# A fourth block of the up projection with seven products for eight, and the remaining units one behind each of most of its steps

## The chip, the cores and the metric

The kernel runs on one core of a Trainium2 chip. Its time is the device time of one execution in microseconds (us). The engines of the core work side by side, each through its own list of instructions in order: TensorE (PE) does the matrix products, VectorE (DVE) and ScalarE (ACT) the elementwise work, GpSimd (POOL) and SyncE (SP) here mostly issue transfers (DMAs). They wait for each other by semaphores. Products accumulate in PSUM, in eight banks of 128x512 values; everything else lies in SBUF, with 128 partitions.

## The reference

One block of an encoder for 256 tokens and 2048 channels: a mixer (retention and latent attention), then an MLP with a squared ReLU. Only the MLP matters here:

```python
D_MODEL = 2048
SEQ = 256
D_FF = 4 * D_MODEL
...
        h = h + _mixer(u, positions, w_in[l], ret_norm_g[l], w_ret_o[l], q_a_norm_g[l],
                       w_q_b[l], kv_a_norm_g[l], w_kv_b[l], w_mla_o[l], w_out[l])
        z = _rmsnorm(h, norm_mlp_g[l]) @ w_up[l]
        h = h + jnp.square(jax.nn.relu(z)) @ w_down[l]
    return _rmsnorm(h, norm_f_g)
```

`w_up` has 2048 x 8192 values, so the up projection turns 256 tokens of 2048 channels into 256 tokens of 8192 hidden channels.

## The kernel before

**Numbers in two halves.** Every fp32 operand is split into a high and a low half in fp32r: ACT casts the value to the high half (`split`, L550), DVE subtracts it from the value and so gets the low half (L551). A product of two such operands is three matmuls: high by high, high by low, low by high. A weight therefore costs, once loaded, one cast on ACT and one subtraction on DVE before PE can use it.

**The up projection in two forms.** The hidden channels are computed in two ways.

A *unit* (`Unit`) yields 128 hidden channels for all 256 tokens. The weights stand in PE and the tokens stream through. It has two parts, of eight tiles of channels each; a part loads 512 KB of weights, splits them, and does eight matmuls 512 wide (L176, high weights by both halves of the tokens) and eight 256 wide (L180, low weights by high tokens). All go into one bank, `z`. After the second part ACT copies the bank out (L1266), DVE adds its halves (L1267), and two parts later ACT applies ReLU and squares (L1270, L1231); POOL issues the store of 128 KB to the hidden units' place in DRAM (`hid`, L1232).

A *block* yields 1024 hidden channels by seven products for eight (Strassen's scheme in Winograd's form on 2x2 blocks: two token halves, two column halves, pairs of channel tiles). It has eight *steps* (`Step`), one for each pair of channel tiles, j = 0 to 7. A step has four parts, 0 to 3. It loads 1 MB in two DMAs (`raw`, `sraw`), forms sums of the weights on DVE (L307, L316, L317, buffer `forms`), and splits four operands, one for each part: the raw pair, two sums each for parts 1 and 2, and one raw tile for part 3. The tokens stand in PE (from `hT`, or their combinations `hc`) and the weights stream. Parts 0 to 3 have two, two, two and one of the seven products, each product three matmuls (L333 to L335). The products add up over the eight steps in seven banks `zs`, numbered 1 to 7; part 0 adds to products 3 and 4, part 1 to 2 and 5, part 2 to 6 and 1, part 3 to 7. With seven of the eight banks held by a block, units and turns share the last one.

At the end of a block `s_end` evicts: four copies on ACT, of products 3, 5, 1 and 7 (L522 to L528, `zo`), and on DVE e = product 6 + copy of 3, f = product 2 - e, product 4 + f and copy of 5 + f (L520); three further operations of DVE follow some parts later. So bank 3 comes free with ACT's first copy, bank 5 with its second, bank 2 with DVE's second operation and bank 4 with its third. The outcome has tokens on partitions, so it is turned: four *turns* for a block (`turn`), each four 128x128 transposes on PE (L1284), a ReLU and a square on ACT and a store of 256 KB. They stand in the next block's steps, from its second step on ahead of part 1; those of the last block stand behind the last two units.

In the kernel before there are three blocks (`SU = 3`, 3072 channels) and 40 units (5120 channels).

**The order.** It is written by hand as a list of parts: three units first (`EARLY`), the blocks' steps with units between, two units last (`LATE`), then the down projection. Units go into *slots* behind part 1 or part 3 of a step; `use` says which slots get one. Before, 23 slots behind part 3 (all but the very last) have a unit, and 12 of the 24 slots behind part 1: the steps with even j. `stream` walks the list: ahead of the matmuls of part n it has the loads up to part n+6 and the preparation (sums, casts and splits) up to part n+4 recorded. Each engine keeps that order. So the copy of a unit's bank stands in ACT's list, and the addition after it in DVE's, behind the preparation of the next four parts, and both hold what is listed behind them until the unit's last matmul is done. The evictions of a block stand likewise behind the preparation of the four parts that follow its last part.

While the first block runs, DVE and ACT also make the remaining half of the combinations `hc` of the tokens (`MAKE`, lines L231 to L241 and a split), which its steps j = 4 to 7 need. These hold two of the five `raw` buffers while they are made.

The down projection then takes the hidden units from DRAM in pairs, those of the units first and those of the blocks after, in steps of the same kinds.

Of the kernel before, what the change touches and what calls it, by code (L numbers as in the profile page):

```python
# [27 lines left out]
CHUNK = 64  # L28
DFF = 8192
FT = DFF // P  # L30
SU = 3
SJ = KT // 2
ST = SU * 1024 // P
EARLY, LATE = 3, 2
AHEAD = 4
PAIRED = 6
MAKE = 7, 2 * EARLY + 18
SUMS = (4, 7, 10), (0, 1, 2)
MANUAL = {getattr(mybir.EngineType, n) for n in ('Activation', 'DVE', 'PE', 'SP', 'Pool')}
# [66 lines left out]
def block_kernel(ctx: ExitStack, tc: tile.TileContext, A):  # L106
# [50 lines left out]
    def wtile(kind, shape):  # L157
        uid[0] += 1
        dt, bufs = (F32, 5) if kind == "raw" else (F32R, 4)
        return wp.tile(shape, dt, tag=kind, bufs=bufs, name=f"{kind}{uid[0]}")  # L160
# [440 lines left out]
    for k in range(KT):  # L601
        t = lead0[:, N_VEC:] if k == 0 else wtile("raw", [P, LEAD])
# [674 lines left out]
    def turn(u, jj):  # L1277
        pT = atps(f"zt{u}{jj}")
        for j in range(2):
            kt = 2 * jj + j  # L1280
            for t in range(2):
                o = j * S + t * P
                src = zo[:, 0, 2 * t + kt // 4, kt % 4 * P : kt % 4 * P + P]
                PE.transpose(pT[:, o : o + P], src, ident)  # L1284
        square(4 * u + jj, pT)

    def step(u, j, qs):
        def end():
            sums = s_end(qs, zo[:, 0].rearrange("p (t c) n -> p t c n", t=2), zo[:, 1])
            next(sums)  # L1290
            later.extend([d, lambda: next(sums)] for d in SUMS[u == SU - 1])
            turns.extend(lambda jj=jj: turn(u, jj) for jj in range(4))
# [13 lines left out]
    early = [Unit(i, 0) for i in range(EARLY)]  # L1306
    parts = [(e, h) for h in range(2) for e in early]
    units = list(range(EARLY, FT - ST - LATE))
    slots = [(u, j, h) for u in range(SU) for j in range(SJ) for h in (1, 3)][:-1]
    whole = [t for t in slots if t[2] == 3]  # L1310
    room = len(units) - len(whole)
    halves = [t for t in slots if t[2] == 1]
    if room >= 0:
        use = set(whole) | {halves[i * len(halves) // room] for i in range(room)}
    else:
        use = {t for t in whole if t[1] != PAIRED or t[0] >= -room}
    for u in range(SU):
        qs = {}
        for j in range(SJ):
# [69 lines left out]
    def finish(half, t, c, n, lo=0, hi=512):  # L1389
        h = residual(half, t, c)[:, lo:hi]  # L1390
        ps = both[half].q[ROLE[t, c]][:, lo:hi]
        V.scalar_tensor_tensor(h, in0=ps, scalar=rh2[:, t : t + 1], in1=h, op0=ALU.mult, op1=ALU.add)

        def square():
            SC.activation(ps, h, AF.Square, accum_out=ssf[:, t, n : n + 1])

        return square
# [90 lines left out]
    with tc.manual_schedule(engines=MANUAL):  # L1488
        stream(parts, after)
        assert not later  # L1490
        for t in range(2):
            for c in range(2):
# [10 lines left out]
                else:  # L1503
                    halves = [finish(1, t, 1, 3, 0, 256)]
# [86 lines left out]
```

## Time and profile before

| what | value |
|---|---|
| time, median of 3 runs | 1566.04 us (1565.64 to 1566.29) |
| the profiled execution | 1566.54 us, its span 1564.8 us |
| PE busy | 1551.3 us (99%) |
| DVE busy | 1316.0 us (84%) |
| ACT busy | 962.6 us (62%) |
| POOL busy | 39.3 us (3%) |
| granted clock of PE, mean | 0.998 |
| from HBM read, to HBM written | 319.72 MB, 12.58 MB |

"Busy" counts the time in which at least one instruction of the engine is under way. In a timeline each row has the start in us from the span's start, the length, the engine, the line of the kernel, the operation, output<-inputs by the program's names (`lo<-raw,hi` is the subtraction that makes a low half), the shape, and xN where N such instructions follow each other; a bracket at the end gives the idle time ahead of it and what ended that. Lengths of matmuls overlap, so the time that one takes from its neighbours is the distance of two starts. The up projection runs from about 878 us, its first unit, to 1222 us.

### The profile page before, as it was taken

What the parts mean: (1) busy time and instruction counts of PE and PEld (TensorE: products, weight loads), DVE (VectorE), ACT (ScalarE), POOL (GpSimd) and SP (SyncE); (2) the same over time, 40 slices, a digit from 0 to 9 for tenths busy, and PEclk for the clock granted to TensorE, in tenths of its full rate; (3) what the DMA queues carried; (4) which work ended last, traced back from release to release, by engine and by line L of the source; (5) the groups of instructions that cost most, each with busy time, mean ns of one, the idle gap of its engine ahead of it and who ended that gap; (6) DMA issues with size and microseconds to landing.
All of it is one profiled execution on the core that took longest, in us unless ns stands there. A gap on an engine that the chain in (4) does not pass through costs nothing.

```text
span 1564.8 us, 21391 instructions
## 1 busy us (share of the span) xinstructions
PE 1551.3 (99%) x7655; PEld 1311.0 (84%) x7655; DVE 1316.0 (84%) x1787; ACT 962.6 (62%) x1416; POOL 39.3 (3%) x76
## 2 busy tenths in 40 slices
PE   9999999999999999999999999999999999999997
PEld 7888888888898888888888888888888888888886
DVE  7898877799976988976567689887978899989996
ACT  6645655566545667875445567676767766656664
POOL 0000000000000000000000000000000100000000
PEclk9999999999999999999999999999999999999999
DMA  9666755566656654444556657666675977686873
GB/s 319 207 203 208 230 164 161 159 201 206 206 168 220 213 197 143 157 136 161 185 206 211 236 196 247 214 226 232 207 249 188 376 265 245 237 304 211 266 255 115
DMA packets 107626, 333.70 MB, mean 213 GB/s; under 512 B 11264, under 2 KB 12160, under 8 KB 106496
## 3 DMA queue, kind: packets, MB, share of 16 engines
q1 hardware_dynamic: 104208, 318.71, 61.1%
q0 software_dynamic: 3168, 11.54, 1.9%
q10 hardware_dynamic: 144, 2.10, 0.4%
q8 instruction: 60, 0.98, 0.3%
q14 instruction: 46, 0.38, 0.1%
HBM read 319.72 MB, written 12.58 MB: 212 GB/s over the span
## 4 chain that ended last, share of the span: by engine, by line
PE 79%; DVE 1%; issue 1%; ACT 1%; DVEq 0%; POOLq 0%; POOL 0%; ACTq 0%
PE z L176 9%; PE dn L358 7%; PE dn L359 7%; PE dn L357 7%; PE z L180 5%; PE zs L333 2%; PE zs L334 2%; PE zs L335 2%; PE mo L214 2%; PE mo L215 2%; PE mo L217 2%; PE wo L214 2%; PE wo L215 2%; PE wo L217 2%; PE gm L357 2%; PE yr L358 2%
## 5 line engine op out<-in xcount | busy, mean ns | idle before, releaser
L551 DVE TENSOR_TENSOR lo<-raw,hi 128x1024 fp32r<-128x1024 f32 (+3 forms) x214 | 232.0, 1101 | 22.7 <-ACT hi L550 22.2
L169 DVE TENSOR_TENSOR lo<-raw,hi 128x1024 fp32r<-128x1024 f32 (+1 forms) x148 | 173.2, 1171 | 89.7 <-ACT hi L168 89.6
L168 ACT CAST hi<-raw 128x1024 fp32r<-128x1024 f32 (+1 forms) x148 | 149.6, 1011 | 155.9 <-PE mo L215 44.9
L550 ACT CAST hi<-raw 128x1024 fp32r<-128x1024 f32 (+3 forms) x214 | 200.0, 953 | 55.3 <-issue 9.5
L551 DVE TENSOR_TENSOR morelo<-raw,morehi 128x1024 fp32r<-128x1024 f32 (+1 forms) x118 | 127.1, 1098 | 18.8 <-ACT morehi L550 18.3
L550 ACT CAST morehi<-raw 128x1024 fp32r<-128x1024 f32 (+1 forms) x118 | 109.1, 949 | 10.5 <-issue 3.2
L550 ACT CAST hi<-forms 128x1024 fp32r<-128x1024 f32 x70 | 73.7, 1052 | 51.2 <-DVE forms L307 28.1
L176 PE MATMUL z<-hT,morehi 128*128 128x512 f32 x408 | 101.6, 391 | 0.0
L357 PE MATMUL dn<-hi,dd 128*128 128x512 f32 x230 | 89.6, 389 | 0.0
L359 PE MATMUL dn<-hi,dd 128*128 128x512 f32 x230 | 89.5, 389 | 0.0
L358 PE MATMUL dn<-lo,dd 128*128 128x512 f32 x230 | 89.5, 389 | 0.0
L551 DVE TENSOR_TENSOR lo<-forms,hi 128x1024 fp32r<-128x1024 f32 x70 | 85.0, 1221 | 5.3 <-ACT hi L550 4.9
L176 PEld LDWEIGHTS z<-hT,morehi 128*128 128x128 f32 x408 | 74.9, 188 | 14.4
L1266 ACT COPY hs<-z 128x512 f32<-128x512 f32 x40 | 23.5, 587 | 71.2 <-PE z L180 71.1
L357 PE MATMUL dn<-morehi,dd 128*128 128x512 f32 x156 | 60.7, 389 | 0.0
L358 PE MATMUL dn<-morelo,dd 128*128 128x512 f32 x156 | 60.7, 389 | 0.0
L359 PE MATMUL dn<-morehi,dd 128*128 128x512 f32 x156 | 60.7, 389 | 0.0
L180 PEld LDWEIGHTS z<-hT,morelo 128*128 128x128 f32 x408 | 55.6, 190 | 4.0
L176 PE MATMUL z<-hT,hi 128*128 128x512 f32 x232 | 57.9, 392 | 0.0
L180 PE MATMUL z<-hT,morelo 128*128 128x256 f32 x408 | 56.9, 282 | 0.0
L307 DVE TENSOR_TENSOR forms<-raw,sraw 128x1024 f32<-128x1024 f32 x46 | 56.1, 1219 | 0.3 <-DMA raw<-w_up_s 0.3
L358 PEld LDWEIGHTS dn<-lo,dd 128*128 128x128 f32 x230 | 43.2, 188 | 9.0
(500 smaller groups left out, 4193.9 us busy)
## 6 DMA issues: line engine op xcount, KB each, us to landing
raw<-w_down SPq DMA_DIRECT2D x106, 512.0 KB, 6.0
raw<-w_up SPq DMA_DIRECT2D x80, 512.0 KB, 5.1
raw<-w_rv SPq DMA_DIRECT2D x32, 512.0 KB, 4.8
raw<-w_rg SPq DMA_DIRECT2D x32, 512.0 KB, 4.3
raw<-w_gret SPq DMA_DIRECT2D x32, 512.0 KB, 4.4
raw<-w_ret_o SPq DMA_DIRECT2D x32, 512.0 KB, 5.0
raw<-w_gmla SPq DMA_DIRECT2D x32, 512.0 KB, 4.3
raw<-w_mla_o SPq DMA_DIRECT2D x32, 512.0 KB, 3.7
```

Source lines behind the costliest of these rows:

```text
L168: SC.copy(hi, raw)
L169: V.tensor_tensor(out=lo, in0=raw, in1=hi.bitcast(F32), op=ALU.subtract)
L176: PE.matmul(out, w[0][:, k], x.both(k0 + k), start=start and k == 0, stop=False)
L180: PE.matmul(out[:, :S], w[1][:, k], x.hi(k0 + k), start=False, stop=stop and k == n - 1)
L214: PE.matmul(out, x.hi(k0 + k, ts), w[0][:, k], start=start and k == 0, stop=False)
L215: PE.matmul(out, x.lo(k0 + k, ts), w[0][:, k], start=False, stop=False)
L217: PE.matmul(out, x.hi(k0 + k, ts), w[1][:, k], start=False, stop=stop and k == nk - 1)
L357: PE.matmul(q, ah, wh, start=start, stop=False)
L358: PE.matmul(q, ah, wl, start=False, stop=False)
L359: PE.matmul(q, al, wh, start=False, stop=self.left[f] == 0)
L550: SC.copy(hi, val)
L551: V.tensor_tensor(out=lo, in0=val, in1=hi.bitcast(F32), op=ALU.subtract)
```

## The change

The number of blocks goes from three to four (`SU`), so 4096 of the 8192 hidden channels come from blocks, in 32 steps, and 32 units are left instead of 40. Three of these stay first and two last; the other 27 are spread over the 31 slots behind part 3 of a step, and no unit stands behind part 1 any more. With whole division by 27 the slots that get none are numbers 7, 15, 23 and 30, counted from 0: behind the last steps of blocks 0, 1 and 2, and behind the seventh step of block 3.

```diff
-SU = 3
+SU = 4
 SJ = KT // 2
 ST = SU * 1024 // P
 EARLY, LATE = 3, 2
 AHEAD = 4
-PAIRED = 6
...
     units = list(range(EARLY, FT - ST - LATE))
-    slots = [(u, j, h) for u in range(SU) for j in range(SJ) for h in (1, 3)][:-1]
-    whole = [t for t in slots if t[2] == 3]
-    room = len(units) - len(whole)
-    halves = [t for t in slots if t[2] == 1]
-    if room >= 0:
-        use = set(whole) | {halves[i * len(halves) // room] for i in range(room)}
-    else:
-        use = {t for t in whole if t[1] != PAIRED or t[0] >= -room}
+    whole = [(u, j, 3) for u in range(SU) for j in range(SJ)][:-1]
+    use = {whole[i * len(whole) // len(units)] for i in range(len(units))}
```

The program up to the up projection keeps its order; line numbers are smaller by one there. In the rows below, `z` is a unit's bank, `zs` a block's, `zo` a block's evicted values, `hi`, `lo`, `morehi` and `morelo` the split weights; "waits" names the engines whose semaphore an instruction waits for ("Activation" is ACT).

PE's list where block 0 ends and block 1 begins, before: the last rows of the unit behind the last step, and then products 3, 4 and 2 of the new block.

```order
L180 MATMUL z14_9272<-hT0_7390,morelo1022_60_9214 128x256 x7
L176 MATMUL z14_9272<-hT1_7391,morehi1022_61_9223 128x512 [waits Activation_49]
L176 MATMUL z14_9272<-hT1_7391,morehi1022_61_9223 128x512 x7
L180 MATMUL z14_9272<-hT1_7391,morelo1022_61_9224 128x256 [waits DVE_49]
L180 MATMUL z14_9272<-hT1_7391,morelo1022_61_9224 128x256 x7
L333 MATMUL zs10333_9318<-morehi1023_62_9239,hT0_7390 128x512 [waits Activation_49]
L334 MATMUL zs10333_9318<-morehi1023_62_9239,hT0_7390 128x512
L335 MATMUL zs10333_9318<-morelo1023_62_9240,hT0_7390 128x512 [waits DVE_49]
L333 MATMUL zs10334_9319<-morehi1023_62_9239,hc0_7713 128x512 [waits Activation_49]
L334 MATMUL zs10334_9319<-morehi1023_62_9239,hc0_7713 128x512
L335 MATMUL zs10334_9319<-morelo1023_62_9240,hc0_7713 128x512
L333 MATMUL zs10332_9320<-hi1025_9253,hc0_7713 128x512 [waits DVE_49]
```

The same place in PE's list now: the last product of the old block, and at once products 3, 4 and 2 of the new one.

```order
L332 MATMUL zs9337_8325<-hi1001_8982,hT1_7391 128x512 [waits Activation_49]
L333 MATMUL zs9337_8325<-hi1001_8982,hT1_7391 128x512
L334 MATMUL zs9337_8325<-lo1002_8983,hT1_7391 128x512 [waits DVE_49]
L332 MATMUL zs10093_9068<-hi1003_9006,hT0_7390 128x512 [waits Activation_49]
L333 MATMUL zs10093_9068<-hi1003_9006,hT0_7390 128x512
L334 MATMUL zs10093_9068<-lo1004_9007,hT0_7390 128x512 [waits DVE_49]
L332 MATMUL zs10094_9069<-hi1003_9006,hc0_7713 128x512 [waits Activation_49]
L333 MATMUL zs10094_9069<-hi1003_9006,hc0_7713 128x512
L334 MATMUL zs10094_9069<-lo1004_9007,hc0_7713 128x512
L332 MATMUL zs10092_9070<-morehi1004_53_9018,hc0_7713 128x512 [waits DVE_49]
L333 MATMUL zs10092_9070<-morehi1004_53_9018,hc0_7713 128x512
L334 MATMUL zs10092_9070<-morelo1004_53_9019,hc0_7713 128x512
```

The unit is gone from between; product 3 now waits for ACT, product 4 for ACT and product 2 for DVE right behind the last matmul of the old block.

DVE's list there, before, from the splits of that unit to the first split behind the evictions (the four rows L520 that write `zo`):

```order
L551 TENSOR_TENSOR morelo1022_60_9214<-raw1016_9161,morehi1022_60_9213 128x1024
L551 TENSOR_TENSOR morelo1022_61_9224<-raw1019_9184,morehi1022_61_9223 128x1024
L307 TENSOR_TENSOR forms_8108<-raw1022_9209,sraw1022_9210 128x1024
L551 TENSOR_TENSOR morelo1023_62_9240<-sraw1022_9210,morehi1023_62_9239 128x1024
L316 TENSOR_TENSOR forms_8108<-forms_8108,sraw1022_9210 128x512
L317 TENSOR_TENSOR forms_8108<-forms_8108,raw1022_9209 128x512
L551 TENSOR_TENSOR lo1026_9254<-forms_8108,hi1025_9253 128x1024
L520 TENSOR_TENSOR zo_8175<-zs9336_8321,zo_8175 128x512
L520 TENSOR_TENSOR zo_8175<-zs9332_8319,zo_8175 128x512
L520 TENSOR_TENSOR zo_8175<-zs9334_8318,zo_8175 128x512
L520 TENSOR_TENSOR zo_8175<-zo_8175 128x512
L551 TENSOR_TENSOR lo1028_9269<-raw1023_9236,hi1027_9268 128x1024
```

And now, from the addition of the unit ahead of the last step:

```order
L1266 TENSOR_TENSOR hs201_9002<-hs201_9002 128x256
L306 TENSOR_TENSOR forms_8108<-raw998_8957,sraw998_8958 128x1024
L550 TENSOR_TENSOR lo1004_9007<-sraw998_8958,hi1003_9006 128x1024
L315 TENSOR_TENSOR forms_8108<-forms_8108,sraw998_8958 128x512
L316 TENSOR_TENSOR forms_8108<-forms_8108,raw998_8957 128x512
L550 TENSOR_TENSOR morelo1004_53_9019<-forms_8108,morehi1004_53_9018 128x1024
L550 TENSOR_TENSOR morelo1005_54_9034<-forms_8108,morehi1005_54_9033 128x1024
L550 TENSOR_TENSOR morelo1006_55_9046<-raw998_8957,morehi1006_55_9045 128x512
L519 TENSOR_TENSOR zo_8175<-zs9336_8323,zo_8175 128x512
L519 TENSOR_TENSOR zo_8175<-zs9332_8321,zo_8175 128x512
L519 TENSOR_TENSOR zo_8175<-zs9334_8320,zo_8175 128x512
L519 TENSOR_TENSOR zo_8175<-zo_8175 128x512
```

The unit's two splits are gone from ahead of the evictions, and the splits for parts 2 and 3 of the next step (the second and third `morelo`) have come in.

PE's list behind part 1 of the very first step, before:

```order
L335 MATMUL zs9335_8320<-lo926_8240,hc0_7713 128x512
L176 MATMUL z3_8357<-hT0_7390,hi927_8262 128x512 x8
L180 MATMUL z3_8357<-hT0_7390,lo928_8263 128x256 x8
L176 MATMUL z3_8357<-hT1_7391,hi929_8285 128x512 x8
L180 MATMUL z3_8357<-hT1_7391,lo930_8286 128x256 x8
L333 MATMUL zs9336_8321<-hi932_8313,hc0_7713 128x512
```

And now:

```order
L334 MATMUL zs9335_8322<-lo924_8236,hc0_7713 128x512
L332 MATMUL zs9336_8323<-hi926_8260,hc0_7713 128x512
L333 MATMUL zs9336_8323<-hi926_8260,hc0_7713 128x512
L334 MATMUL zs9336_8323<-lo927_8261,hc0_7713 128x512
L332 MATMUL zs9331_8324<-hi926_8260,hT0_7390 128x512
L333 MATMUL zs9331_8324<-hi926_8260,hT0_7390 128x512
```

Parts 2 and 3 of the step follow part 1 at once, and the unit stands behind part 3.

## The prediction

> **What bounds the kernel now.** I read the page first, for the engine that is busy throughout, then the waits of that engine, then the window of the stage that is edited, and last the timelines of TensorE (PE), VectorE (DVE) and ScalarE (ACT) in it.
>
> ```profile
> span 1564.8 us, 21391 instructions
> PE 1551.3 (99%) x7655; PEld 1311.0 (84%) x7655; DVE 1316.0 (84%) x1787; ACT 962.6 (62%) x1416; POOL 39.3 (3%) x76
> ```
>
> The waits of PE in the whole program (us in total, times, longest):
>
> ```profile
> PE spin L573 <- DVE cold L570: 1.2, 1, 1.2
> PE first L622 <- DVE x L554: 1.1, 2, 0.6
> PE ms L1022 <- DVE k L541: 1.0, 1, 1.0
> PE my L584 <- DVE pp L551: 0.7, 1, 0.7
> ```
>
> The up projection's stretch by engine (us, busy and count; granted clock; DMA share; GB/s):
>
> ```profile
> 878.00:1222.00 344.00, 344.00 (x1839) 296.78 (x1838) 290.77 (x333) 235.75 (x337) 26.23 (x48) 1.00 0.66 225
> ```
>
> PE is busy for 99% of the span, and its four waits, 4.0 us in all, lie elsewhere: the first two at the start, the others in the attention. In the 344 us of the up projection PE never stands still. So PE's work is the time there, and a microsecond of it saved is one gained, as long as DVE keeps up. DVE is at 290.77 of 344 us (85%), ACT at 235.75: DVE is the engine to watch. The profiled execution took 1566.54 us around this span, 0.5 us more than the median of the runs, 1566.04.
>
> **The change part by part.** A block of 1024 columns turns from eight units into eight steps, the evictions at its end and four turns. The prices on PE, from the start of one piece to the start of the next:
>
> ```profile
> 990.55 0.40 PE L333 MATMUL zs<-hi,hT 128*128 128x512 f32 x1
> ...
> 995.34 1.98 PE L176 MATMUL z<-hT,morehi 128*128 128x512 f32 x8
> ...
> 1000.90 0.40 PE L333 MATMUL zs<-morehi,hT 128*128 128x512 f32 x1
> ...
> 1002.29 0.39 PE L333 MATMUL zs<-hi,hc 128*128 128x512 f32 x1
> ...
> 1016.83 0.40 PE L333 MATMUL zs<-hi,hT 128*128 128x512 f32 x1
> ...
> 1018.23 0.60 PE L1284 MATMUL zt<-con,zo 128*128 128x128 f32 x4
> ...
> 1022.12 1.98 PE L176 MATMUL z<-hT,morehi 128*128 128x512 f32 x8
> ```
>
> A step (four parts, 21 matmuls) lasts 990.55 to 995.34, 4.79 us; a unit 995.34 to 1000.90, 5.56 us; a step with a turn in it (the four 128x128 transposes at 1018.23) 1016.83 to 1022.12, 5.29 us, so a turn costs 0.50 us. Eight units removed are 44.5 us, eight steps added 38.3 us, four turns 2.0 us: **PE's own work falls by 4.2 us.** The weights read are the same bytes in as many DMAs of 512 KB on SP, and four fewer stores of the hidden units go out on POOL, whose wait for them holds nobody on PE: nothing for either.
>
> On DVE the trade goes the other way:
>
> ```profile
> 984.09 1.22 DVE L307 TENSOR_TENSOR forms<-raw,sraw 128x1024 f32<-128x1024 f32 x1
> ...
> 987.69 2.43 DVE L551 TENSOR_TENSOR lo<-forms,hi 128x1024 fp32r<-128x1024 f32 x2
> 990.03 0.68 DVE L551 TENSOR_TENSOR lo<-raw,hi 128x512 fp32r<-128x512 f32 x1
> 991.37 0.43 DVE L1267 TENSOR_TENSOR hs<-hs 128x256 f32<-128x256 f32 x1 [0.66 <-ACT hs L1266]
> 992.32 2.36 DVE L551 TENSOR_TENSOR morelo<-raw,morehi 128x1024 fp32r<-128x1024 f32 x2 [0.52 <-ACT morehi L550]
> 994.60 1.22 DVE L307 TENSOR_TENSOR forms<-raw,sraw 128x1024 f32<-128x1024 f32 x1
> ...
> 998.20 1.22 DVE L551 TENSOR_TENSOR lo<-forms,hi 128x1024 fp32r<-128x1024 f32 x1
> 999.34 2.14 DVE L520 TENSOR_TENSOR zo<-zs,zo 128x512 f32<-128x512 f32 x3
> 1001.39 0.68 DVE L520 TENSOR_TENSOR zo<-zo 128x512 f32<-128x512 f32 x1
> ```
>
> An operation lets the next one start 0.08 us before its end (a full split: 998.20 to 999.34, 1.14, at a length of 1.22). A step's preparation runs from 984.09 (first sum of weights) to the last split, 990.03, and 0.60 for this, in all 6.54 us; a unit's two splits take 994.60 less 992.32, 2.28 us, and the addition after its copy 0.34 (0.43 long). Eight units less are 21.0 us, eight steps more 52.3 us, and one more set of seven evicting operations at 0.68 (three of them are the 2.14 at 999.34) 4.8 us. DVE goes from 290.8 to about 327 us in a stretch that PE would leave at 340: 96%. DVE still fits on the average, so the question is where it is late.
>
> *Between blocks.* The four slots that the spreading leaves without a unit are numbers 7, 15, 23 and 30 of 31: the first three are exactly the ends of blocks 0, 1 and 2. There the last step of a block is followed at once by the first step of the next, whose products need the banks that the evictions free. DVE's order puts all four splits of that next step ahead of the evictions. In the trace of before, the same place has a unit between, and the evictions come after the splits of two parts only. ACT's rows there, the copy that evicts the unit before the last step and the first evicting copies:
>
> ```profile
> 990.75 0.59 ACT L1266 COPY hs<-z 128x512 f32<-128x512 f32 x1 [1.38 <-PE z L180]
> ...
> 996.87 0.58 ACT L522 COPY zo<-zs 128x512 f32<-128x512 f32 x1
> 997.34 0.59 ACT L524 COPY zo<-zs 128x512 f32<-128x512 f32 x1
> ```
>
> The copy starts at 990.75, 0.20 us after the last step's first matmul (990.55), and DVE's addition at 991.37 waits for it. In before DVE then does a unit's splits (up to 994.60), the next step's first sum and so on to its second split (998.20), and the evictions at 999.34; the second of the three, which frees the bank of product 2, ends at 999.34 + 0.68 + 0.69 = 1000.71. PE needs that bank at 1002.29: 1.6 us to spare. In the changed order the unit's splits fall away there (994.60 less 991.71, where the addition has let go: 2.89 us) and the third and the fourth split come in ahead of the evictions (1.20 us, from the pair at 987.69 to 990.03 less 1.14, and 0.60). The subtraction then ends at 1000.71 - 2.89 + 1.80 = 999.62, or 9.07 us after the last step's first matmul. PE is there after one step (4.79) and the six matmuls of the next one's first part (1000.90 to 1002.29, 1.39), 6.18 us. **It waits 2.9 us, three times: 8.7 us.** Part of it is already spent ahead of the first part, whose bank waits for ACT's first copy (996.87); that copy comes after four casts instead of two, and is inside the same 2.9. The lower end is 2.2, if the addition did not have to wait for the copy (its idle time at 991.37 is 0.66); the upper 4.0, if DVE comes a microsecond late into the boundary. I take 2.9, from the rows of the same place. Behind a boundary a cycle of one step and one unit costs PE 10.35 us, and DVE 6.54 + 2.28 + 0.34 plus 0.95 from the start of the addition to the unit's first split (991.37 to 992.32, of which 0.34 is the addition), some 9.8: it catches up by half a microsecond a cycle, and seven cycles lie between boundaries.
>
> The clock of PE bears on those waits:
>
> ```profile
> 1.19 3.59 PE L573 MATMUL spin<-cold 128*128 128x512 bf16 x8 [1.19 <-DVE cold L570]
> ```
>
> ```profile
> 1550.00:1564.80 14.80, 5.76 (x26) 4.44 (x24) 4.90 (x11) 4.30 (x10) 1.06 (x2) 0.82 0.38 142
> ```
>
> The eight matmuls with which the program begins take 3.59 us, eight of the same width in a unit 1.98 (995.34): a cold start costs 1.6 us. The granted clock is 1.00 in the whole stage and falls only in the tail, to 0.82, where PE is busy for 5.76 of 14.80 us. A wait of 2.9 us in two pieces lies between the 1.2 us that PE waited once with no lower clock and these 9.0 idle ones; I put no clock loss into the sum and keep it as rival 4. [...]
>
> *The opening.* The first block loses the units that stood after the first part pair of its first and third step, while DVE there also makes the remaining combinations of activations:
>
> ```profile
> 892.55 1.22 DVE L551 TENSOR_TENSOR lo<-forms,hi 128x1024 fp32r<-128x1024 f32 x1
> ...
> 898.30 1.22 DVE L551 TENSOR_TENSOR lo<-forms,hi 128x1024 fp32r<-128x1024 f32 x1 [1.25 <-ACT hi L550]
> ...
> 901.29 1.23 DVE L551 TENSOR_TENSOR morelo<-raw,morehi 128x1024 fp32r<-128x1024 f32 x1 [1.02 <-ACT morehi L550]
> ...
> 935.13 1.22 DVE L231 TENSOR_TENSOR raw<-hT 128x1024 f32<-128x1024 f32 x1
> ...
> 938.54 0.42 DVE L237 TENSOR_TENSOR raw<-raw 128x256 f32<-128x256 f32 x1
> ...
> 947.18 1.22 DVE L551 TENSOR_TENSOR hc<-raw,hc 128x1024 fp32r<-128x1024 f32 x1
> ```
>
> ```profile
> 895.78 0.40 PE L333 MATMUL zs<-morehi,hT 128*128 128x512 f32 x1
> ```
>
> ```profile
> 921.21 1.05 ACT L550 CAST hi<-raw 128x1024 fp32r<-128x1024 f32 x1 [0.87 <-DMA raw<-w_up]
> ```
>
> From 892.55 (second split of the first step) to the second split of the sixth step DVE now has to do: the rest of the first step 2.9, four steps 26.2, five units 11.4, eight additions 2.7, two sets of combinations (1.14 for the row at 935.13, 1.14 for 947.18, four of 0.4 like 938.54) 7.8, and 4.7 of the sixth step: 55.7 us, so up to 948.2. PE, from 895.78, comes to that split after five steps (24.0), five units (27.8), a first part (1.39) and two matmuls (0.46), at 949.4. That leaves 1.2 us for waiting; DVE's waits for ACT at 898.30 and 901.29 alone are 2.3 us, and the cast at 921.21 waited 0.87 us for its weights. It comes late by 1.1 to 2.0 us. Ends: nothing (the waits at the start overlap the lead), and 3 us (if the two raw buffers that the combinations hold delay a load a second time). I take 1.5.
>
> *The end.* After the last block, two steps without a unit between stand before the last two units. DVE, from the copy: 0.62, 0.34, one step 6.54, four splits of units 4.56, four evictions 2.7: 14.8 us; PE's first turn comes after two steps and a unit less 0.2, 14.9. That is even; I put 0.2, ends nothing and 0.5. The down projection has DVE as ready as before.
>
> Sum: -4.2 + 8.7 + 1.5 + 0.2 = **+6.2 us**. From the profiled 1566.5 that is 1572.7, and 0.5 lower beside the median: **1572.2 us**.
>
> **The rivals.** (1) *The boundaries are hidden, and it is faster.* The subtraction would have to end within 1.4 us of PE's need, since three times that is the 4.2 gained. It speaks for it that DVE waits 0.66 us at 991.37 and so has time in hand; against it that this wait is for the very copy from which the chain is counted. With no wait at all and no loss in the opening: 1566.0 - 4.2 = 1561.8. (2) *About the same.* The boundaries at 1.4 to 2.2 and the opening at nothing: 1566 to 1568.6. (3) *DVE is full in every cycle.* Two additions one cycle apart:
>
> ```profile
> 1017.65 0.43 DVE L1267 TENSOR_TENSOR hs<-hs 128x256 f32<-128x256 f32 x1
> 1018.00 0.69 DVE L520 TENSOR_TENSOR zo<-zo 128x512 f32<-128x512 f32 x1
> ...
> 1028.49 0.43 DVE L1267 TENSOR_TENSOR hs<-hs 128x256 f32<-128x256 f32 x1
> ```
>
> They lie 10.84 us apart with a turn in the cycle and no idle time before the second, where PE's cycle is 10.85. If DVE needs those 10.84 without a turn too, PE loses 0.5 in some 15 plain cycles: 7 us on top, 1579. Against it: 0.6 of them went to a late eviction (1018.00), which only two cycles of a block have. (4) *The clock falls at the boundaries.* Then each costs what the cold start does, 1.6 us more, three times 4.8: 1577. It decides at some length between the 1.2 us that cost nothing and the tail's 9.0, so a boundary of 2.9 may be past it; against it stands that the six matmuls of the first part cut that wait in two. [...]
>
> **How the numbers follow.** Forecast 0.71 (1569.2 to 1576), rival 1 0.08, rival 2 0.08, rival 3 0.05, rival 4 0.08. About 0.2%, 3.1 us, is what a measurement of this kernel can tell from no change: below 1562.9 is faster, 0.08; rival 2 is the same, 0.08; the rest is slower, 0.84. The range takes the low ends (3 x 2.2 - 4.2 = +2.4: 1568.4) and the high ones (12.0 + 3.0 + 0.5 - 4.2 = +11.3: 1577.3).
>
> **What would show it.** Right: new waits of PE on the matmuls of the steps (L332 to L334) for ACT's and DVE's evictions of the last block, three places, some 2.9 us each; a stretch of about 350 us from the first unit to the first product of the down projection; DVE busy near 327 us in it; PE's waits for splits in the first 75 us of it, 1 to 2 us; the granted clock at 1.00 there. Wrong: no wait at the boundaries, or the loss spread over all cycles, or a loss in the down projection, which I leave as it is.

## The result

The changed kernel takes 1573.94 us (median of 6 runs, 1573.01 to 1576.21), the one before 1566.0: the ratio is 1.0055, with an interval of 1.0044 to 1.0067. The forecast was 1572.2 us, slower, within 1568.4 to 1577.3.

The profile after: the page's first lines, the waits of PE, and the stretch of the up projection by engine (columns as in the prediction; the stage is now a line number lower).

```profile
span 1572.1 us, 21324 instructions
PE 1547.7 (98%) x7583; PEld 1303.3 (83%) x7583; DVE 1350.2 (86%) x1826; ACT 971.9 (62%) x1420; POOL 36.9 (2%) x72
```

```profile
PE zs L332 <- ACT zo L521: 6.4, 3, 2.3
PE zs L334 <- DVE morelo L550: 1.8, 1, 1.8
PE zs L332 <- DVE zo L519: 1.6, 3, 0.5
```

```profile
878.00:1228.00 350.00, 340.25 (x1755) 288.27 (x1754) 323.35 (x370) 244.28 (x340) 23.64 (x44) 1.00 0.65 218
```

PE is busy for 1547.7 us, 3.6 less than before, in a span that is 7.3 longer. Three rows of waits are new in the up projection: three waits for ACT's first evicting copy (L521), three for DVE's evictions (L519), and one for a split. DVE is busy for 323.4 us there, where 327 were worked out, and the granted clock is 1.00. To place the loss, the down projection's first matmul in the trace of before:

```profile
1222.27 0.48 PE L357 MATMUL dn<-hi,dd 128*128 128x512 f32 x1
```

And in the trace of the changed kernel, the first step's first matmul, then the down projection's first:

```profile
895.64 0.40 PE L332 MATMUL zs<-morehi,hT 128*128 128x512 f32 x1
```

```profile
1229.59 0.48 PE L356 MATMUL dn<-hi,dd 128*128 128x512 f32 x1
```

From the one to the other it is 333.95 us now, and 1222.27 less 895.78, 326.49 us, before: 7.5 us more, which is the whole difference of the spans, 7.3. The down projection gives nothing back and takes nothing.

The first block end, on PE, then on DVE and on ACT. PE's last step of block 0 begins at 970.22; the bracket is the wait.

```profile
970.22 0.40 PE L332 MATMUL zs<-morehi,hT 128*128 128x512 f32 x1
...
974.78 0.39 PE L334 MATMUL zs<-lo,hT 128*128 128x512 f32 x1
977.51 0.50 PE L332 MATMUL zs<-hi,hT 128*128 128x512 f32 x1 [2.34 <-ACT zo L521]
...
978.77 0.40 PE L334 MATMUL zs<-lo,hc 128*128 128x512 f32 x1
979.69 0.51 PE L332 MATMUL zs<-morehi,hc 128*128 128x512 f32 x1 [0.53 <-DVE zo L519]
...
983.27 1.98 PE L175 MATMUL z<-hT,hi 128*128 128x512 f32 x8
```

```profile
971.36 0.42 DVE L1266 TENSOR_TENSOR hs<-hs 128x256 f32<-128x256 f32 x1
...
975.29 2.42 DVE L550 TENSOR_TENSOR morelo<-forms,morehi 128x1024 fp32r<-128x1024 f32 x2
977.63 0.69 DVE L550 TENSOR_TENSOR morelo<-raw,morehi 128x512 fp32r<-128x512 f32 x1
978.23 2.13 DVE L519 TENSOR_TENSOR zo<-zs,zo 128x512 f32<-128x512 f32 x3
```

```profile
970.42 0.59 ACT L1265 COPY hs<-z 128x512 f32<-128x512 f32 x1 [0.32 <-PE z L179]
...
976.88 0.58 ACT L521 COPY zo<-zs 128x512 f32<-128x512 f32 x1
```

DVE's addition at 971.36, the splits of four parts, the last at 977.63, and only then the evictions at 978.23: the order that was read off the list. PE starts its last matmul of the old block at 974.78 and then stands, does part 0 at 977.51 when ACT's copy (976.88) is done, stands again, and goes on at 979.69 when the subtraction has ended. The pair of steps that should take 9.58 us, two times 4.79, takes 13.05 (to 983.27); at the other two block ends it takes 12.77 and 12.78. The second end on PE, the two waits, the matmul behind the second of them, and the unit:

```profile
1059.82 0.50 PE L332 MATMUL zs<-hi,hT 128*128 128x512 f32 x1 [2.03 <-ACT zo L521]
...
1062.01 0.50 PE L332 MATMUL zs<-hi,hc 128*128 128x512 f32 x1 [0.52 <-DVE zo L519]
1062.35 0.40 PE L333 MATMUL zs<-hi,hc 128*128 128x512 f32 x1
...
1065.61 1.98 PE L175 MATMUL z<-hT,morehi 128*128 128x512 f32 x8
```

The rows of waits add up to 8.0 us at the three ends, the pairs of steps to 9.9 too much. A row counts from the modelled end of the matmul before, 0.39 us behind its start, where the next one could have started after 0.23; and the first matmul behind a wait holds PE for 0.34 us (1062.01 to 1062.35). So the starts show the loss, and the rows most of it.

The opening, where the third step of block 0 (916.34 to 923.20, 6.86 us) waits for the low half of part 1, and what DVE waited for ahead of that split:

```profile
920.12 0.50 PE L334 MATMUL zs<-morelo,hc 128*128 128x512 f32 x1 [1.78 <-DVE morelo L550]
```

```profile
914.10 1.23 DVE L306 TENSOR_TENSOR forms<-raw,sraw 128x1024 f32<-128x1024 f32 x1 [1.20 <-DMA raw<-w_up_s]
...
918.85 2.35 DVE L550 TENSOR_TENSOR morelo<-forms,morehi 128x1024 fp32r<-128x1024 f32 x2
```

Put together, from starts of pieces on PE:

| term | predicted | measured |
|---|---|---|
| PE's own work | -4.2 | -4.5 |
| three block ends | 8.7 | 3.47 + 3.19 + 3.20 = 9.9 |
| opening | 1.5 | 2.07 + 0.07 = 2.1 |
| end of the last block | 0.2 | 0.0 |
| sum | 6.2 | 7.5 |

PE's own work is what is left of the 7.5 when the waits are taken out. The 0.3 more that it saves is the twelve steps that a unit no longer cuts in two: a whole one takes 4.79 us, a cut one 2.75 and 2.07.

### The profile page after: what moved, and what is told of

Read it like the earlier page. It is cut to its first block, busy times and chain, and to the rows that moved or that the text cites. A ratio compares the mean times of both kernels' runs of the same rounds, so it can differ in the third digit from the quotient of the medians.

```text
span 1572.1 us, 21324 instructions
## 1 busy us (share of the span) xinstructions
PE 1547.7 (98%) x7583; PEld 1303.3 (83%) x7583; DVE 1350.2 (86%) x1826; ACT 971.9 (62%) x1420; POOL 36.9 (2%) x72
## 3 DMA queue, kind: packets, MB, share of 16 engines
q0 software_dynamic: 3104, 11.54, 1.8%
## 4 chain that ended last, share of the span: by engine, by line
PE 76%; DVE 3%; ACT 1%; issue 1%; DVEq 0%; POOLq 0%; POOL 0%; ACTq 0%
PE z L175 7%; PE dn L358 7%; PE dn L356 7%; PE dn L357 7%; PE z L179 4%; PE zs L332 3%; PE zs L333 3%; PE zs L334 3%; PE mo L214 2%; PE mo L213 2%; PE mo L216 2%; PE wo L214 2%; PE wo L213 2%; PE wo L216 2%; PE gm L356 2%; PE yr L357 2%
## 5 line engine op out<-in xcount | busy, mean ns | idle before, releaser
L550 DVE TENSOR_TENSOR lo<-raw,hi 128x1024 fp32r<-128x1024 f32 (+3 forms) x236 | 252.5, 1085 | 33.0 <-ACT hi L549 32.4
L549 ACT CAST hi<-raw 128x1024 fp32r<-128x1024 f32 (+3 forms) x236 | 218.0, 941 | 61.3 <-issue 7.9
L550 DVE TENSOR_TENSOR morelo<-raw,morehi 128x1024 fp32r<-128x1024 f32 (+1 forms) x88 | 93.3, 1079 | 5.6 <-ACT morehi L549 5.6
L549 ACT CAST morehi<-forms 128x1024 fp32r<-128x1024 f32 x50 | 52.6, 1053 | 58.0 <-DVE forms L316 28.2
L549 ACT CAST morehi<-raw 128x1024 fp32r<-128x1024 f32 (+1 forms) x88 | 80.8, 937 | 6.1 <-issue 2.1
L175 PE MATMUL z<-hT,hi 128*128 128x512 f32 x296 | 73.9, 392 | 0.0
L175 PEld LDWEIGHTS z<-hT,hi 128*128 128x128 f32 x296 | 54.2, 188 | 10.4
L550 DVE TENSOR_TENSOR morelo<-forms,morehi 128x1024 fp32r<-128x1024 f32 x50 | 60.9, 1221 | 0.8
L175 PE MATMUL z<-hT,morehi 128*128 128x512 f32 x216 | 53.7, 391 | 0.0
L358 PEld LDWEIGHTS dn<-hi,dd 128*128 128x128 f32 x240 | 45.1, 188 | 9.4
```

Of the source, the lines that this page charges most:

```text
L175: PE.matmul(out, w[0][:, k], x.both(k0 + k), start=start and k == 0, stop=False)
L358: PE.matmul(q, al, wh, start=False, stop=self.left[f] == 0)
L549: SC.copy(hi, val)
L550: V.tensor_tensor(out=lo, in0=val, in1=hi.bitcast(F32), op=ALU.subtract)
```

## The experiments

The theory: the empty slots at the block ends cost 3.3 us each, because the evictions stand in DVE's and ACT's lists behind the preparation of four further parts; the opening costs 2.1 us for want of two units; and four blocks as such fit. The rival: DVE, at 323 of 350 us, has too much to do for four blocks, and would be late somewhere wherever the units stand. In each case the time beside it is that of the kernel before in the same comparison.

**The block ends filled.**

```diff
-    use = {whole[i * len(whole) // len(units)] for i in range(len(units))}
+    use = set(whole) - {(1, 4, 3), (2, 2, 3), (2, 5, 3), (3, 4, 3)}
```

> The changed kernel with the four slots without a unit put elsewhere: behind steps (block 1, j=4), (2, 2), (2, 5) and (3, 4), so that each block end has a unit behind it. Theory (banks late at the block ends): the three waits of PE for the evictions vanish, and with them the 9.9 us by which those three pairs of steps are longer than 9.58; an empty slot inside a block costs 0 to 0.5 us; total 1564 to 1566. Rival (DVE is too full for four blocks, wherever the empty slots are): the lateness comes back at the new empty slots, total 1571 to 1574.

Measured: 1564.51 us (1563.48 to 1567.13; before 1566.33; ratio 0.9991, interval 0.9983 to 1.0000). The waits of PE, where of the three rows in the steps one is left:

```profile
PE zs L334 <- DVE morelo L550: 1.8, 1, 1.8
```

The waits for evictions are gone: the two steps with an empty slot between take 10.02 us with one turn, 10.52 with two, that is 9.58 and the turns. What is left of lateness is small: the second steps of blocks 1 to 3 take 5.50, 5.49 and 5.55 us where a step with a turn takes 5.29, since the turn there waits for ACT's copy of the unit's bank, too shortly for the rows above. Four blocks fit DVE but for that; where the empty slots stand is what costs. The median is 1.8 us below the kernel before, with an interval that ends at no change: of the 4.5 us that PE saves the opening takes 2.1 and these steps 0.7. The profiled execution, at 1566.78, also had a fall of the granted clock in the opening (last section).

**The opening filled.**

```diff
     use = {whole[i * len(whole) // len(units)] for i in range(len(units))}
+    use = use - {(2, 3, 3), (3, 3, 3)} | {(0, 0, 1), (0, 2, 1)}
```

> The changed kernel with two units put back behind part 1 of the first and third step of block 0, taken from behind steps (2, 3) and (3, 3); the block ends stay empty. Theory (DVE late in the opening for want of those two units): the wait of 1.8 us in the third step goes, the waits at the block ends stay as they are, total 2.1 us below the changed kernel, 1571 to 1572. Rival (DVE too full): the waits only move, total 1574 as before this edit.

Measured: 1571.85 us (before 1566.33; ratio 1.0041, 1.0027 to 1.0055), 2.1 below the changed kernel, as the theory has it.

```profile
PE zs L332 <- ACT zo L521: 6.1, 3, 2.0
PE zs L332 <- DVE zo L519: 1.0, 2, 0.5
```

The wait for the split is gone; those at the block ends are nearly as they were (6.1 us for ACT, where the changed kernel has 6.4). The pairs of steps there take 12.74, 12.72 and 13.78 us. The first is 0.3 shorter than in the changed kernel, so its lateness came from the opening; the third is 1.0 longer by a fall of the clock (last section). That the 2.1 is met to a tenth is partly luck: the five runs go from 1571.35 to 1574.88.

**Both.**

```diff
-    use = {whole[i * len(whole) // len(units)] for i in range(len(units))}
+    use = set(whole) - {(u, j, 3) for u in (1, 2, 3) for j in (2, 5)} | {(0, 0, 1), (0, 2, 1)}
```

> Both edits together: a unit behind each block end and two behind part 1 in the first block, six empty slots behind j=2 and j=5 of blocks 1 to 3. Theory: only the 4.2 us that PE saves are left, less 0 to 0.5 us for each empty slot: 1562 to 1564, below the kernel before (1566.0). Rival (DVE too full): 1569 or more.

Measured: 1562.58 us (1561.86 to 1562.87; before 1566.33; ratio 0.9976, interval 0.9966 to 0.9985). All waits of PE, and its stretch of the up projection:

```profile
PE spin L572 <- DVE cold L569: 1.2, 1, 1.2
PE first L621 <- ACT hi L549: 1.1, 2, 0.7
PE ms L1021 <- DVE k L540: 1.0, 1, 1.0
PE first L621 <- DVE x L553: 0.8, 1, 0.8
PE my L583 <- DVE pp L550: 0.7, 1, 0.7
```

```profile
890.00:1215.00 325.00, 324.88 (x1674) 276.54 (x1674) 312.43 (x355) 234.82 (x326) 23.42 (x43) 1.00 0.68 226
```

No row of waits is left in the up projection, in which PE is busy for 324.88 and DVE for 312.43 of 325 us, 96%. This is faster than both kernels, by 3.7 us than the one before. Of the 4.5 us that PE saves, 0.1 goes for the two steps that are cut again, and some 0.9 for short waits in four steps: the sixth of block 0, where a split of DVE is late (5.01 us instead of 4.79), and the second of blocks 1 to 3, whose turn waits for ACT to copy the unit's bank (5.49, 5.55 and 5.55 instead of 5.29). The rest arrives. The rival, a loss wherever the units stand, falls, but for these 0.9.

**The kernel before with empty block ends.**

```diff
         use = set(whole) | {halves[i * len(halves) // room] for i in range(room)}
+        use = use - {(0, 7, 3), (1, 7, 3)} | {(0, 5, 1), (1, 5, 1)}
```

> The kernel before, with three blocks, where the units behind the last steps of blocks 0 and 1 stand behind part 1 of the sixth step (j=5) of the same blocks instead. Theory: the empty block ends alone make it slower, by 3.3 us each, 6.6 in all: 1572.6, with the same two pieces of wait (for ACT's copy, then for DVE's subtraction) as in the changed kernel. Rival (it takes DVE's load of four blocks to make the wait): DVE is at 85% here, no change, 1566.

Measured: 1573.08 us (before 1566.33; ratio 1.0044, 1.0030 to 1.0058), 6.75 us slower, 3.4 for each of the two ends.

```profile
PE zs L333 <- ACT zo L522: 3.4, 2, 1.7
PE zs L333 <- DVE zo L520: 2.6, 2, 1.3
```

Here with three blocks DVE has some 15% of its time free in the stage, and still the two pieces of wait are there at both ends. The second piece is longer than in the changed kernel (1.3 instead of 0.5), since behind the first two parts of the next step comes a unit here: its two whole splits stand ahead of the evictions, in place of a whole and a half one. The empty block end is enough by itself; the fourth block is not needed for it.

**The evictions earlier, and later.** The block ends stay empty. In `stream`, at the end of a block with no unit behind it, two parts are prepared ahead of the evictions instead of four, and in the other kernel five:

```diff
             ahead = AHEAD if n else 2
+            if type(it) is Step and it.j == SJ - 1 and h > 1 and type(parts[n + 4 - h][0]) is Step:
+                ahead = 5 - h
```

```diff
             ahead = AHEAD if n else 2
+            if type(it) is Step and it.j == SJ - 1 and h > 2 and type(parts[n + 1][0]) is Step:
+                ahead = 5
```

> The changed kernel, its empty block ends kept, but at these ends the evictions stand ahead of the splits for parts 2 and 3 of the next step in the lists of DVE and ACT (two parts of preparation ahead of them instead of four, as they stand in the kernel before). Theory (the wait is the chain in the lists: preparation of four parts, then evictions): the subtraction ends 1.8 us earlier, so the wait for evictions falls from 2.7 to about 1.1 us at each end; the split of part 2, now behind the evictions, comes 0.6 us late instead; each end costs about 2.2 instead of 3.3 us, total 3 to 4 us below the changed kernel, 1570 to 1571. Rival (DVE as a whole has too much to do there): the sum of the waits at an end stays, 1574.

> The changed kernel with the preparation of five parts ahead of the evictions at the three empty block ends, one more than it has: a unit's first split goes ahead of them. Theory: each wait grows by that split, 1.14 us, 3.4 in all: 1577.3; where the granted clock falls behind a wait (it did once, for 3.4 us at half, in the first experiment's profile), 1.6 us more each time, so up to 1582. Rival: the wait is set by something else than DVE's list, no change, 1574.

Measured: 1569.83 us with the evictions earlier and 1579.77 with them later (before 1565.94; ratios 1.0028, 1.0018 to 1.0037, and 1.0092, 1.0078 to 1.0106). PE's waits in the steps with the evictions earlier:

```profile
PE zs L332 <- DVE zo L521: 2.8, 3, 0.9
PE zs L334 <- DVE morelo L552: 2.1, 3, 1.5
PE zs L334 <- DVE lo L552: 0.3, 1, 0.3
```

And with the evictions later:

```profile
PE zs L332 <- ACT zo L523: 9.2, 3, 3.3
PE zs L334 <- DVE morelo L552: 2.0, 1, 2.0
PE zs L332 <- DVE zo L521: 1.4, 2, 0.7
```

With two parts ahead the waits for evictions are 2.8 us in all instead of 8.0, and the pairs of steps take 11.86, 11.64 and 11.54 us, which is 2.1 a block end instead of 3.3, with the split of part 2 late instead (0.5 us each by PE's starts; the second row's 1.5 is the opening). With five ahead they are 10.6 us (the row of 2.0 is the opening), and the pairs take 14.14, 14.42 and 13.91: 4.6, 4.8 and 4.3 too much, the second with a fall of the clock in it. So the place of the evictions in the list sets the wait: a fifth part ahead costs 1.1 us more at the first and the third end, the 1.14 of a split, and two parts less give 1.2 back of the 1.8 that their splits take, since the split of part 2 is then late itself. The later kernel's median is above the forecast 1577.3 by 2.5 and inside what was put down for falls of the clock, up to 1582. Its profiled execution, at 1578.05, had one such fall (below). The mean granted clock of each run says that the others had more: 0.997 in that one, then 0.996 at 1579.02, 0.995 at 1579.77, 0.993 at 1580.96 and 0.992 at 1581.86, where one fall is worth 0.001 (3.4 us at half, in a span of 1576).

**One set of combinations earlier.**

```diff
-MAKE = 7, 2 * EARLY + 18
+MAKE = -1, 2 * EARLY + 18
...
-        if c in (1, 2):
+        if c:
             for _ in hc.make(c - 1):
```

> The changed kernel with the third set of token combinations made in the output projection's last quarter instead of in the first block; the fourth stays. Theory (in the opening DVE has 3.8 us too much ahead of the third step, partly waiting for weights while that set holds two raw buffers): the wait of 1.8 us there goes, total 2.1 us below the changed kernel, 1571.8; the block ends keep their 9.9 us. Rival: the work is paid where it goes, with waits of PE in the output projection, 1574.

Measured: 1571.85 us (before 1565.94; ratio 1.0038, 1.0026 to 1.0051), 2.1 below the changed kernel.

```profile
PE zs L332 <- ACT zo L521: 6.1, 3, 2.0
PE ms L1021 <- DVE k L540: 1.0, 1, 1.0
PE zs L332 <- DVE zo L519: 1.1, 2, 0.5
```

The wait in the opening is gone and no new one stands in the output projection. So either two units more or that set less cures the opening. The pairs of steps at the block ends take 13.48, 12.73 and 12.73 us; the first has a fall of the clock in it, so here too the tenth is luck. Whether DVE's own work or the buffers that the set holds (the load that came 1.20 us late at 914.10) make the lateness in the opening is not told apart: this edit takes away both.

## Why the prediction was right

*The saving of 4.2 us* was right: 4.5 in the changed kernel, and the kernel with both places filled is 3.7 below the one before. What the sum left out is the 0.03 us that each of twelve cut steps had cost.

*The block ends* were right in place, chain and number. The term was sized 2.9 and measured 3.5, 3.2 and 3.2. The end of the subtraction was put 9.07 us behind the last step's first matmul, and PE's product 2 started 9.17 and 9.16 us behind it at the second and third end (1052.84 to 1062.01 at the second), 3.0 late. What was missed is 0.3: 0.1 up to that start, and 0.2 behind it, where PE takes 3.60 us for the rest of the step (1062.01 to 1065.61) that takes 3.40 elsewhere. Half of that is the first matmul. At the first end DVE came 0.3 us late besides, still behind from the opening: it ended its last split there and added at 971.36, at once, where the copy at 970.42 would have allowed 971.04; with the opening filled, this end takes 12.74 us like the others. The prediction had this lateness only in its upper bound.

*The opening* was right that DVE would be late by one to two microseconds, but not where: it was put at the sixth step, and PE waited in the third. The step of the working that failed is the sum over five steps, which lets the waits of DVE spread over the whole stretch. They stand at its head: 1.2 us for a load at 914.10, and before that 1.28 and 0.48 us for ACT (splits at 898.17 and 899.88), so the lead was gone after two steps. After that there is only 0.07 us of loss in the sixth. The term was 1.5 and measured 2.1; that it came so near for another place is partly luck.

*The end of the last block* at 0.2 cost nothing.

*The rivals.* That the block ends would be hidden, or cost 2.2 us or less with nothing lost in the opening, is ruled out by the changed kernel's own waits. That DVE is full in every cycle falls with the kernel that fills both places: DVE at 96%, and no row of waits. That the clock falls at the waits did not happen in the changed kernel's profiled execution, but it did in four of the experiments'. The prediction's price for it, 1.6 us, was met in one of them, the opening of the kernel with filled ends. At the block ends it was 1.0 (13.78 us instead of 12.74), 0.75 (13.48 instead of 12.73) and 0.3 to 0.5 us (14.42 instead of 14.14 and 13.91): there the slower matmuls use up part of a wait that comes next anyway (by PE's starts that wait, for DVE's subtraction, is 0.67 to 0.69 us at the changed kernel's three ends, 0.33 in the first of these and gone in the other two). The prediction's other bound, 1.2 us of waiting without a lower clock, shows nothing: that wait stands ahead of the eight slow matmuls at the start, before the clock first rose (at 6.54 us in the trace of before). Of the changed kernel's six runs, the two at 1576 have a mean clock of 0.997, but so have two of those at 1574, so what made these two slower isn't settled.

## What to carry to other kernels

When work is spread evenly, look which slots whole division leaves empty: here they fell on the three places where a bank had to be given back, and there a slot is worth 3.3 us. The slots tried inside later blocks are worth nothing, and two in the opening 2.1 together. A prefetch distance counted in parts also sets how late the other instructions of an in-order engine run: evictions recorded after the prefetch wait for it, and need the more cover on the bounding engine the longer the prefetch is (2.1, 3.3 and some 4.4 us lost without cover at two, four and five parts). A trade that makes the bounding engine's work shorter and a second engine's longer (here 85% to 96%) can arrive nearly in full, but only after each place where the second engine holds something back has been given its cover.

## What the runs showed of the hardware that was not expected

The granted clock of PE fell to a half after waits as short as 1.8 us, in some executions and not in others. In the opening it stayed at 1.00 in the changed kernel, with a wait of 1.78 us, and fell in the kernel with filled block ends, behind one of 1.80. PE's rows there, and the stretch by engine (the granted clock is the third number from the end).

```profile
918.27 0.39 PE L333 MATMUL zs<-morehi,hc 128*128 128x512 f32 x1
920.46 0.64 PE L334 MATMUL zs<-morelo,hc 128*128 128x512 f32 x1 [1.80 <-DVE morelo L550]
920.90 0.63 PE L332 MATMUL zs<-morehi,hc 128*128 128x512 f32 x1
...
923.46 0.63 PE L332 MATMUL zs<-morehi,hT 128*128 128x512 f32 x1
923.88 0.49 PE L333 MATMUL zs<-morehi,hT 128*128 128x512 f32 x1
924.21 0.40 PE L334 MATMUL zs<-morelo,hT 128*128 128x512 f32 x1
```

```profile
918.00:920.00 2.00, 0.66 (x3) 0.20 (x2) 2.00 (x3) 1.77 (x3) 0.00 (x0) 1.00 0.69 283
920.00:922.00 2.00, 1.54 (x4) 1.26 (x5) 2.00 (x3) 2.00 (x3) 0.00 (x0) 0.67 0.76 231
922.00:924.00 2.00, 2.00 (x6) 1.54 (x6) 2.00 (x4) 1.62 (x4) 0.33 (x1) 0.50 0.45 107
924.00:926.00 2.00, 2.00 (x10) 1.67 (x9) 2.00 (x3) 0.34 (x2) 0.21 (x1) 0.98 1.04 291
```

Matmuls follow at 0.42 us (923.46 to 923.88) instead of 0.23 until 923.88, and the step takes 8.47 us instead of the changed kernel's 6.86: 1.6 us for the fall. By the four stretches the clock was at half for 1.32, 2.00 and 0.08 us, 3.4 in all. In the traces' records of the clock each of the four falls below lasts 3.413 us at 0.50, and begins a whole multiple of 3.413 us after the clock's first rise at the program's start. In those of before and of the changed kernel, where it falls only in the tail, it stands at 1.00 for 1553.06 and 1563.30 us from that rise, which is 455 and 458 times 3.4133. I cut the span into windows of this length from the rise and took from PE's starts (a 512-wide matmul at 0.23 us) how long it stood idle in each:

| kernel | wait of PE, us | idle in the window with most of it, of 3.413 | clock |
|---|---|---|---|
| changed, block end 1 | 975.01 to 977.51 | 1.67 | stays |
| changed, block end 2 | 1057.63 to 1059.82 | 1.23, and 0.67 of the second piece | stays |
| changed, block end 3 | 1139.97 to 1142.16 | 1.65, and 0.28 of the second piece | stays |
| before with empty ends, end 2 | 1111.55 to 1113.40 | 1.85 | stays |
| opening filled, end 1 | 983.45 to 985.63 | 1.84 | stays |
| later evictions, end 3 | 1142.77 to 1145.90 | 1.83, and 0.09 of the second piece | stays |
| ends filled, opening | 918.50 to 920.46 | 1.96 | half from 920.66 |
| opening filled, end 3 | 1142.46 to 1144.65 | 2.19 | half from 1145.71 |
| one set earlier, end 1 | 972.47 to 974.66 | 2.18 | half from 974.65 |
| later evictions, end 2 | 1058.77 to 1061.90 | 3.13 | half from 1062.15 |

In all four falls the window that has just ended held 1.96 us or more in which PE stood idle, and in none of the other rows did one hold more than 1.93. So in these ten rows it is not the wait's length alone that counts but how it lies to these windows: a wait of 2.2 us fell into one window twice, and the clock fell; the other times an edge cut it, and the clock stayed. In one of the falls the window was idle for 1.96 of its 3.413 us, 57%, and PE had worked for the rest of it. Where the bound lies, if idle time alone sets it, isn't settled: 1.93 and 1.96 us are close, and if the 0.1 us by which the first matmul behind a wait is longer is counted as idle as well, windows with up to 2.03 us kept the clock.
